# The first LayerNorm of an encoder block: rows normalized by ScalarE in one pass, factor and offset applied behind the transposes

## The chip, the cores and the metric

One core of a Trainium2 chip. The metric is the device time of one execution in microseconds (us), the median of the runs shown; lower is better. Engines are named as the profile names them: PE (TensorE), PEld (its weight loads), DVE (VectorE), ACT (ScalarE), POOL (GpSimd), SP (SyncE, which here only issues DMAs).

## What is computed

One encoder layer on 256 tokens of width 1024, in float32. Cut to what the change touches:

```python
h = layer_norm(x, ln_in_g, ln_in_b)          # 256 x 1024
mem_n = layer_norm(mem, ln_mem_g, ln_mem_b)
mix = mixer_branches(h, mem_n, ...)          # h @ w_in + b_in, three branches, gates, w_out, + b_out
h = layer_norm(DN_ALPHA * h + mix, ln1_g, ln1_b)
ff = moe_ffn(h, ...)                         # top-4 of 32 experts
out = layer_norm(DN_ALPHA * h + ff, ln2_g, ln2_b)
```

## The kernel before

The kernel has two halves. `mixer` runs from the start to about 306 us. It multiplies the transposed rows with the columns of `w_in` and with the branch weights. Each float32 operand is split into a high part (`hi`, rounded by ACT) and a low part (`lo`, the remainder, by DVE; both in `split`, L117 and L118), and `mm3` (L144 to L146) makes three matmuls of each product. `moe` runs after that and streams 403 MB of expert weights through ring buffers of 2 MB on the SP queue; the first units of the ring are loaded from inside the mixer (`early_load`).

The work around the change, in order:

- **The first LayerNorm** (L230 to L301). The 256 rows come as two tiles `xs[0]` and `xs[1]` of 128 x 1024, with factor `g` and offset `b` spread over 128 partitions (512 KB each). DVE makes the statistics; POOL raises the variance to -1/2 (L63) and DVE refines it (L69 to L74). Then each row tile is finished in pieces: ACT and POOL do columns 768 to 1023 (L283 to L285), DVE columns 0 to 511 (L287, L290) and 512 to 767 (L293, L294). The result `hs[tau]` is the normalized row tile with factor and offset; it is kept for the residual.
- **The transposes.** PE turns blocks of 128 x 128 of `hs` into PSUM tiles `tps` of 128 x 512 (one for each half `j` of the columns and each row tile `tau`), and `split` takes each straight from PSUM into `hT`.
- **The first matmuls.** The strip `wlr` of `w_in` (32 columns, its parts split at the end of the start) is multiplied with `hT` in 24 matmuls into `pj`; then follow the chunks of 128 columns of `w_in`, 24 matmuls each.
- **Small vectors.** `brow` gathers biases and LayerNorm vectors as 74 rows of 128; PE transposes it (L366) so that `bT` holds each as a column per partition.
- **The memory's LayerNorm** (`mem_norm_gen`, `mem_turn_gen`) already has the other form: ACT normalizes whole rows, and behind the transposes four ACT instructions (L399) put factor and offset on, since there they are one value per partition.
- **The residual** (`residual_gen`, L662). ACT multiplies `hs` by ALPHA (L665) and POOL adds `b_out` (L666).
- **The end of the mixer** (`ev_o`). DVE adds the projection to `hs`, makes the statistics and normalizes (L771, L772) while POOL computes the power.

Background work is written as generators that are stepped between the chunks of the matmuls (`bg.tick`); each `yield` names a number of microseconds of background work, which paces the generators. In the start, in the last projection and in the expert half the order on DVE and PE is written by hand (`manual_schedule`, which at the start takes ACT too); elsewhere a scheduler orders each engine's queue by its own model. Each engine runs its queue strictly in order. The weights in `wraw` have 3 buffers, the split parts `whi` and `wlo` 4 each, so ACT and DVE can run several chunks ahead of PE.

## Time and profile before

| | us |
|---|---|
| median of 3 runs | 1235.38 (1235.21 to 1237.03) |
| the profiled execution: its own time | 1235.43 |
| its span, first to last instruction | 1233.5 |
| busy: PE, DVE, ACT, POOL | 1168.8, 381.5, 259.0, 47.4 |
| moved by DMA | 458.24 MB |

The profiled execution lies 0.05 us from the median, and its span 1.9 us below its own time. Busy time is summed over the whole span; which engine waits for which differs by stage, so the stages are read one by one.

### The profile page before, as it was taken

The numbers are of one execution on the slowest core, as the hardware profiler recorded it, in microseconds if no ns is written. First come the engines' busy times: TensorE is split into PE (matmuls) and PEld (weight loads), VectorE is DVE, ScalarE is ACT, GpSimd is POOL, SyncE is SP. The second block draws the span as 40 slices with busy tenths as digits, with TensorE's granted clock in tenths as the row PEclk, the third lists the DMA queues.
The fourth block names the chain that finished last, engine by engine and source line by source line (L and its number), as shares of the span: only waits on it lengthen the run. The fifth ranks groups of instructions, "written<-read, shape, count | busy, mean of one in ns | idle before, by whom it ended". The sixth has DMA issues, their size and how long they took to land.

```text
span 1233.5 us, 14884 instructions
## 1 busy us (share of the span) xinstructions
PE 1168.8 (95%) x6413; PEld 639.0 (52%) x6413; DVE 381.5 (31%) x591; ACT 259.0 (21%) x453; POOL 47.4 (4%) x70
## 2 busy tenths in 40 slices
PE   7999999999999999999998989899989989898995
PEld 6898999998533443434333343334342424242432
DVE  7995565487212131120202121012111111111124
ACT  4775555453111010100101010201010101010110
POOL 2150000000000000000000000000000000000000
PEclk8999999999999999999999999899999999999998
DMA  8755557687999999999999999999999999999993
GB/s 283 258 195 172 188 196 247 257 308 271 372 378 431 425 431 431 428 431 431 430 430 432 431 430 430 431 430 430 430 430 430 431 430 430 431 429 431 429 421 129
DMA packets 74921, 458.24 MB, mean 371 GB/s; under 512 B 4662, under 2 KB 39040, under 8 KB 50148
## 3 DMA queue, kind: packets, MB, share of 16 engines
q1 hardware_dynamic: 74392, 456.62, 90.1%
q8 instruction: 52, 0.85, 0.3%
q10 hardware_dynamic: 332, 0.56, 0.2%
q14 instruction: 17, 0.14, 0.0%
q0 software_dynamic: 128, 0.07, 0.0%
HBM read 456.18 MB, written 1.05 MB: 371 GB/s over the span
## 4 chain that ended last, share of the span: by engine, by line
PE 66%; DMA 29%; DVE 2%; ACT 1%; issue 0%; SPq 0%; POOL 0%; DVEq 0%; ACTq 0%
DMA wexp<-in_w_down_dram 25%; PE gps L1004 19%; PE yps L1004 13%; PE pj L146 7%; PE pj L144 7%; PE pj L145 6%; PE mps L847 5%; DMA wexp<-in_w_gu_dram 3%; PE gps L998 2%; PE yps L1074 1%; PE mps L1074 1%; PE gps L1043 1%; DVE wlo L118 1%; PE yps L998 0%; PE mps L1121 0%
## 5 line engine op out<-in xcount | busy, mean ns | idle before, releaser
L1004 PE MATMUL gps<-wexp,xT 128*64 128x512 f32 x1984 | 441.6, 596 | 7.1 <-DMA wexp<-in_w_gu_dram 7.0
L1004 PEld LDWEIGHTS gps<-wexp,xT 128*64 128x64 f32 x1984 | 145.3, 137 | 299.0 <-issue 280.9
L1004 PE MATMUL yps<-wexp,work 128*64 128x512 f32 x960 | 234.5, 622 | 32.3 <-DMA wexp<-in_w_down_dram 32.3
L1004 PEld LDWEIGHTS yps<-wexp,work 128*64 128x64 f32 x960 | 71.4, 142 | 192.7 <-issue 143.8
L809 DVE TENSOR_SCALAR sg<-gps 128x512 f32<-128x512 f32 x31 | 21.3, 687 | 424.1 <-PE gps L1004 390.8
L118 DVE TENSOR_TENSOR wlo<-wraw,whi 128x1024 fp32r<-128x1024 f32 (+2 forms) x98 | 119.3, 1227 | 61.8 <-ACT whi L117 61.1
L810 ACT ACTIVATE sg<-sg 128x512 f32<-128x512 f32 x32 | 20.2, 630 | 460.0 <-DVE sg L809 459.9
L117 ACT ACTIVATE whi<-wraw 128x1024 fp32r<-128x1024 f32 (+2 forms) x98 | 95.4, 978 | 97.4 <-PE pj L145 80.2
L144 PE MATMUL pj<-hT,whi 128*128 128x256 f32 (+1 forms) x392 | 112.5, 287 | 0.0
L145 PE MATMUL pj<-hT,whi 128*128 128x256 f32 (+1 forms) x392 | 110.5, 282 | 0.3 <-DVE hT L118 0.3
L146 PE MATMUL pj<-hT,wlo 128*128 128x256 f32 (+1 forms) x392 | 110.5, 282 | 0.0
L1050 DVE SCALAR_TENSOR_TENSOR y<-yps,sw,y 128x512 fp32r<-128x512 f32 x30 | 22.5, 751 | 230.3 <-ACT y L1049 229.3
L145 PEld LDWEIGHTS pj<-hT,whi 128*128 128x128 f32 (+1 forms) x392 | 73.6, 188 | 1.0 <-DVE hT L118 0.8
L144 PEld LDWEIGHTS pj<-hT,whi 128*128 128x128 f32 (+1 forms) x392 | 73.6, 188 | 0.8 <-ACT whi L117 0.7
L146 PEld LDWEIGHTS pj<-hT,wlo 128*128 128x128 f32 (+1 forms) x392 | 73.5, 188 | 0.2
L1049 ACT ACTIVATE y<-yps,sw 128x512 fp32r<-128x512 f32 x30 | 20.6, 687 | 233.5 <-PE yps L1004 226.0
L847 PEld LDWEIGHTS mps<-P,h 128*128 128x128 f32 x512 | 61.6, 196 | 12.7 <-issue 12.2
L847 PE MATMUL mps<-P,h 128*128 128x128 f32 x512 | 64.8, 285 | 0.4 <-DVE P L840 0.4
L1078 DVE TENSOR_TENSOR sum<-sum,yps 128x512 f32<-128x512 f32 (+1 forms) x30 | 18.8, 666 | 71.6 <-PE yps L1074 71.6
L995 POOL COPY sel<-kp 128x128 f32<-128x128 f32 x32 | 9.4, 295 | 806.4 <-PE yps L998 450.5
L938 ACT ACTIVATE xT<-mps 128x512 f32<-128x512 f32 x32 | 19.1, 597 | 58.9 <-PE mps L847 58.9
L812 DVE TENSOR_TENSOR sg<-sg 128x512 f32<-128x512 f32 x32 | 22.1, 690 | 3.2 <-ACT sg L810 1.6
(275 smaller groups left out, 1045.9 us busy)
## 6 DMA issues: line engine op xcount, KB each, us to landing
wexp<-in_w_gu_dram SPq DMA_DIRECT2D x127, 2048.0 KB, 35.5
wexp<-in_w_down_dram SPq DMA_DIRECT2D x60, 2048.0 KB, 29.0
wraw<-in_w_in_dram SPq DMA_DIRECT2D x28, 1024.0 KB, 5.4
wexp<-in_w_down_dram SPq DMA_DIRECT2D x8, 768.0 KB, 17.3
wraw<-in_w_mem_kv_dram SPq DMA_DIRECT2D x4, 1024.0 KB
wraw<-in_w_br_gla_dram SPq DMA_DIRECT2D x4, 1024.0 KB
wraw<-in_w_out_dram SPq DMA_DIRECT2D x4, 1024.0 KB, 7.5
wraw<-in_w_br_fnet_dram SPq DMA_DIRECT2D x2, 1024.0 KB
```

The lines of the kernel that those rows point to most:

```text
L117: K.nc.scalar.activation(hi, src, AF.Copy)
L118: K.nc.vector.tensor_tensor(lo, src, hi.bitcast(F32), ALU.subtract)
L144: nc.tensor.matmul(out, wh, xh, start=first, stop=False)
L145: nc.tensor.matmul(out, wh, xl, start=False, stop=False)
L146: nc.tensor.matmul(out, wl, xh, start=False, stop=last)
L809: nc.vector.tensor_scalar(g, gate, 7.0, None, ALU.min)
L812: nc.vector.tensor_tensor(g, g, s, ALU.mult)
L847: nc.tensor.matmul(t[:, c], h1[tau][:, f0 + c % 2:f0 + 256:2], P[:, tau].rearrange("p e s -> p (e s)"), start=first and c == 0, stop=last, ...
L998: nc.tensor.matmul(ac, t[r].rearrange("k e s -> k (e s)"), bias[r, c0:c0 + ac.shape[-1]], start=first, stop=not first, skip_group_check=True)
L1004: nc.tensor.matmul(acc[e * 64:e * 64 + 64], xT[:, k, e * 64:e * 64 + 64], w[e], start=first, stop=last, skip_group_check=True)
L1050: nc.vector.scalar_tensor_tensor(y[:, 1, sl], acc, w, y[:, 0, sl].bitcast(F32), ALU.mult, ALU.subtract)
L1074: nc.tensor.matmul(c, G[:, tau * 128:tau * 128 + 128], y[:, i, sl], start=i == 0, stop=i == 1)
```

## The change

- The first LayerNorm's rows are normalized by ACT alone, one instruction of 128 x 1024 per row tile, without factor and offset. The DMAs of `g` and `b` and the pieces on DVE and POOL go.
- `brow` grows to 90 rows, with the first LayerNorm's factor and offset in rows 74 to 89, and its transpose moves to the start. Four of its pieces now come by DMAs from ACT's queue, four from POOL's; the two of `blr` go to POOL's as well.
- Behind each group of transposes a new function `turn_affine` puts factor and offset on, block by block of 128 x 128: blocks 0 and 2 on ACT, 1 and 3 on DVE, into a tile of SBUF from which `split` then takes both parts. The split of `wlr` moves behind the four turns. The memory's rows use the same function, on ACT alone as before.
- `hs` now lacks factor and offset. The residual is finished later, on DVE: `b_out`, the factor and the offset come by three DMAs of 512 KB from POOL's queue, and five DVE instructions of 128 x 1024 take the place of two of ACT and two of POOL. The residual's `yield`s now count 6 us instead of 0.
- At the end of the mixer the first of the two normalizing instructions is cut in two halves of 512 columns.

```diff
-    xs, g, b = [first[:, 0], first[:, 1]], first[:, 2], first[:, 3]
+    xs = [first[:, 0], first[:, 1]]
...
-    nc.sync.dma_start(g, A["ln_in_g"][None, :].broadcast_to([128, D]))
-    nc.sync.dma_start(b, A["ln_in_b"][None, :].broadcast_to([128, D]))
...
+    def turn_affine(x, tau, T, j, gc, bc, t, both):
+
+        ps = K.ps.tile([128, 4, 128], F32, name="tps", tag="ms")
+        for c in range(4):
+            nc.tensor.transpose(ps[:, c], x[:, (j * 4 + c) * 128:(j * 4 + c + 1) * 128], K.ident)
+        for c in range(4):
+            ga, ba = [bT[:, o + j * 4 + c:o + j * 4 + c + 1] for o in (gc, bc)]
+            if both and c % 2:
+                V.tensor_scalar(t[:, c], ps[:, c], ga, ba, ALU.mult, ALU.add)
+            else:
+                act.activation(t[:, c], ps[:, c], AF.Identity, bias=ba, scale=ga)
+        sl = slice(tau * 128, tau * 128 + 128)
+        split(K, t, T.hi[j][:, :, sl], T.lo[j][:, :, sl])
...
-            act.activation(hs[tau][:, c], xs[tau][:, c], AF.Identity, bias=t, scale=rs_[tau])
-            gp.tensor_tensor(hs[tau][:, c], hs[tau][:, c], g[:, c], ALU.mult)
-            gp.tensor_tensor(hs[tau][:, c], hs[tau][:, c], b[:, c], ALU.add)
-            c = half[0]
-            V.scalar_tensor_tensor(hs[tau][:, c], xs[tau][:, c], mvs[tau][:, 0:1], g[:, c], ALU.subtract, ALU.mult)
...
+            V.scalar_tensor_tensor(t, m[:, 0:1], -1.0, r, ALU.mult, ALU.mult)
+            act.activation(hs[tau], xs[tau], AF.Identity, bias=t, scale=r)
+        psb = K.ps.tile([128, 90], F32, name="psb", tag="ms")
+        nc.tensor.transpose(psb, brow, K.ident[:90, :90])
+        V.tensor_copy(bT, psb)
+        for j in range(2):
+            for tau in range(2):
+                t = first[:, 2 + j, tau * 512:tau * 512 + 512].rearrange("p (c n) -> p c n", c=4)
+                turn_affine(hs[tau], tau, hT, j, 74, 82, t, True)
         wlr_parts = [K.wspl.tile([128, 1024], F32R, name=n, tag=n)[:, :384].rearrange("p (k n) -> p k n", k=8)
...
-        for j in range(2):
-            for tau in range(2):
-                transpose_split(K, hs[tau], tau, hT, j)
...
+        for i, src in ((1, A["b_out"]), (2, A["ln_in_g"][None, :]), (3, A["ln_in_b"][None, :])):
+            late_rows.append(at_part(i, (D,), part3))
+            nc.gpsimd.dma_start(late_rows[-1], src.broadcast_to([128, D]))
...
-        for tau in range(2):
-            nc.scalar.activation(hs[tau], hs[tau], AF.Copy, scale=ALPHA)
-            nc.gpsimd.tensor_tensor(hs[tau], hs[tau], bo, ALU.add)
-            yield 0
+        bo, g, b = late_rows
+        nc.vector.scalar_tensor_tensor(bo, b, ALPHA, bo, ALU.mult, ALU.add)
+        yield 1.2
+        for tau in range(2):
+            nc.vector.scalar_tensor_tensor(hs[tau], hs[tau], ALPHA, g, ALU.mult, ALU.mult)
+            yield 1.2
+            nc.vector.tensor_tensor(hs[tau], hs[tau], bo, ALU.add)
+            yield 1.2
...
-                nc.vector.scalar_tensor_tensor(hs[tau], hs[tau], mv_[:, 0:1], g1, ALU.subtract, ALU.mult)
+                for c in (slice(0, 512), slice(512, D)):
+                    nc.vector.scalar_tensor_tensor(hs[tau][:, c], hs[tau][:, c], mv_[:, 0:1], g1[:, c], ALU.subtract,
+                                                   ALU.mult)
```

**The start.** ACT's queue before the change, from the normalized columns to the first chunk of weights; `h_68` and `h_69` are the two row tiles `hs`, and the brackets name the semaphore that the instruction waits for.

```order
L283 ACTIVATE h_68<-first,nmr,rsy 128x256 [waits DMAHW0_49,DVE_49]
L283 ACTIVATE h_69<-first,nmr,rsy 128x256 [waits DMAHW4_49,DVE_49]
L117 ACTIVATE whi<-wraw 128x8x32 [waits DMAHW5_49]
L117 ACTIVATE whi<-wraw 128x8x16
L117 ACTIVATE hT<-tps 128x4x128 [waits PE_49] x4
L117 ACTIVATE whi<-wraw 128x1024 [waits DMAHW6_49]
```

ACT's queue with the change, from the rows over the first of the four turns to the start of the second, and the end of the fourth.

```order
L294 ACTIVATE h_68<-first,nmr,rsy 128x1024 [waits DMAHW0_49,DVE_49]
L294 ACTIVATE h_69<-first,nmr,rsy 128x1024 [waits DMAHW4_49,DVE_49]
L278 ACTIVATE first<-tps,bT 128x128 [waits DVE_49,PE_49]
L278 ACTIVATE first<-tps,bT 128x128 [waits DVE_49]
L117 ACTIVATE hT<-first 128x4x128 [waits DVE_49]
L278 ACTIVATE first<-tps,bT 128x128 [waits PE_49]
...
L117 ACTIVATE hT<-first 128x4x128 [waits DVE_49]
L117 ACTIVATE whi<-wraw 128x8x32 [waits DMAHW7_49]
L117 ACTIVATE whi<-wraw 128x8x16
```

DVE's queue with the change at the same place, the first and the fourth turn; the two L276 of a turn are its blocks 1 and 3.

```order
L297 COPY bT<-psb 128x90 [waits PE_49]
L276 TENSOR_SCALAR first<-tps,bT 128x128 [waits Activation_49] x2
L118 TENSOR_TENSOR hT<-first,hT 128x4x128 [waits Activation_49]
...
L276 TENSOR_SCALAR first<-tps,bT 128x128 [waits Activation_49] x2
L118 TENSOR_TENSOR hT<-first,hT 128x4x128 [waits Activation_49]
L118 TENSOR_TENSOR wlo<-wraw,whi 128x8x32 [waits DMAHW7_49,Activation_49]
L118 TENSOR_TENSOR wlo<-wraw,whi 128x8x16 [waits Activation_49]
```

Before, each of the four `hT<-tps` on ACT waited for PE alone, and the split of `wlr` stood ahead of them. Now a block on one engine waits for the block before it on the other, and the split of `wlr` stands last.

**The residual on POOL.** POOL's queue before, around 58 to 86 us; `gla` holds the decayed queries and keys of the gated attention, `parts` a scratch tile.

```order
L581 MEMSET parts 128x512 [waits DVE_49,Activation_49]
L581 MEMSET parts 128x512
L482 TENSOR_TENSOR gla<-gla,parts 128x1024 [waits DMASW1_49,DMASW2_49,DMASW0_49,DMASW3_49,PE_49,Activation_49]
L483 TENSOR_TENSOR gla<-gla,parts 128x1024 [waits Activation_49,Pool_49]
L581 MEMSET parts 128x512 [waits DVE_49]
L581 MEMSET parts 128x512
L666 TENSOR_TENSOR h_68<-h_68,parts_116 128x1024 [waits DMAHW3_49]
L666 TENSOR_TENSOR h_69<-h_69,parts_116 128x1024
L482 TENSOR_TENSOR gla<-gla,parts 128x1024 [waits Activation_49]
L483 TENSOR_TENSOR gla<-gla,parts 128x1024 [waits Activation_49]
```

The same stretch of POOL's queue with the change.

```order
L610 DMA parts_114<-in_b_out_dram 128x1024 [waits DMASW2_49,DVE_49]
L575 MEMSET parts 128x512 [waits DVE_49,Activation_49]
L575 MEMSET parts 128x512
L474 TENSOR_TENSOR gla<-gla,parts 128x1024 [waits DMASW1_49,DMASW6_49,DMASW0_49,DMASW7_49,PE_49,Activation_49]
L475 TENSOR_TENSOR gla<-gla,parts 128x1024 [waits Activation_49,Pool_49]
L575 MEMSET parts 128x512 [waits DVE_49]
L575 MEMSET parts 128x512
L474 TENSOR_TENSOR gla<-gla,parts 128x1024 [waits Activation_49]
L475 TENSOR_TENSOR gla<-gla,parts 128x1024 [waits Activation_49]
```

The two L666 are gone, and the second L482 and L483 (now L474 and L475) follow the memsets directly.

**The residual on DVE.** DVE's queue with the change, around 152 us of the run before; L62 to L74 refine the second row tile's power for the gated attention, and `parts_114` holds `b_out`, factor and offset.

```order
L62 TENSOR_SCALAR ve<-oss 128x4 [waits Activation_49]
L71 TENSOR_TENSOR rst<-rsy 128x4 [waits Pool_49]
L72 TENSOR_TENSOR rst<-rst,ve 128x4 [waits DVE_49]
L660 SCALAR_TENSOR_TENSOR parts_114<-parts_114 128x1024 [waits DMASW3_49,DMASW2_49]
L73 TENSOR_SCALAR rst<-rst 128x4 [waits DVE_49]
L118 TENSOR_TENSOR wlo<-wraw,whi 128x1024 [waits PE_49,Activation_49]
L74 TENSOR_TENSOR rsy<-rsy,rst 128x4 [waits DVE_49]
L682 SCALAR_TENSOR_TENSOR parts<-pj,bT,parts 128x256 [waits Activation_49]
L606 TENSOR_TENSOR parts<-parts,rsy 128x1024 [waits DVE_49]
```

L660, which waits for two DMAs of POOL's queue (`DMASW`), now stands in front of a chunk's `wlo`; the four others of the residual (two L663, two L665) follow within the next 13 rows of that queue.

## Rows read from the trace of the kernel before

**Rows 1.** The page: the chain that ended last, by engine

```profile
PE 66%; DMA 29%; DVE 2%; ACT 1%; issue 0%; SPq 0%; POOL 0%; DVEq 0%; ACTq 0%
```

**Rows 2.** Windows: us; PE, PEld, DVE, ACT, POOL busy; granted clock; DMA share; GB/s

```profile
320.00:330.00 10.00, 10.00 (x48) 3.34 (x48) 0.00 (x0) 0.54 (x1) 0.00 (x0) 1.00 0.77 290
...
560.00:1200.00 640.00, 600.13 (x2815) 238.10 (x2816) 104.62 (x173) 59.17 (x126) 6.56 (x22) 0.97 1.01 430
```

**Rows 3.** Waits of PE from 20 to 310 us: total, times, longest

```profile
PE pj L146 <- DVE wlo L118: 0.4, 2, 0.2
```

**Rows 4.** Timeline of the start: start, length, engine, line, operation, [idle before]

```profile
4.90 4.64 PE L272 MATMUL idle<-kp 128*128 128x128 f32 x20 [4.90 <-DMA kp<-in_c_keep_dram]
...
8.24 0.21 DVE L69 SCALAR_TENSOR_TENSOR rst<-rsy,ve 128x1 f32<-128x1 f32 x1
8.40 0.55 POOL L63 TENSOR_TENSOR rsy<-ve,mh 128x1 f32<-128x1 f32 x1 [1.54 <-DVE ve L62]
...
8.87 0.16 DVE L282 SCALAR_TENSOR_TENSOR nmr<-bmv,rsy 128x1 f32<-128x1 f32 x1
9.06 0.60 ACT L283 ACTIVATE h<-first,nmr,rsy 128x256 f32<-128x256 f32 x1 [7.03 <-DVE nmr L282]
...
13.54 0.62 ACT L117 ACTIVATE whi<-wraw 128x256 fp32r<-128x256 f32 x2 [1.51 <-DMA wraw<-in_w_in_dram]
...
17.09 2.47 DVE L118 TENSOR_TENSOR hT<-tps,hT 128x512 fp32r<-128x512 f32 x4
...
18.66 0.41 PE L146 MATMUL pj<-hT,wlo 128*48 128x256 f32 x1
...
21.77 0.23 PE L366 MATMUL psb<-kp,brow 74*128 74x74 f32 x1
```

**Rows 5.** Windows of the start: columns as in rows 2

```profile
17.50:19.80 2.30, 1.96 (x10) 1.43 (x9) 2.30 (x5) 1.92 (x4) 2.30 (x5) 0.50 0.56 150
19.80:22.00 2.20, 2.20 (x21) 2.20 (x19) 2.07 (x3) 2.20 (x3) 0.71 (x2) 1.00 1.05 367
```

**Rows 6.** Durations: by form (mean ns after the bar); L399's shortest, median, longest ns

```profile
L386 ACT ACTIVATE m<-m,nmr,rsy 128x1024 f32<-128x1024 f32 x2 | 2.5, 1248 | 0.4 <-DVE nmr L385 0.3
L399 ACT ACTIVATE parts<-tps,bT x16: 437/484/528, 61.8 to 69.9; 128x128 f32<-128x128 f32 x16
L428 ACT ACTIVATE gla<-gla 128x512 f32<-128x512 f32 x4 | 2.3, 632 | 0.0
L449 DVE TENSOR_SCALAR parts<-pj,bT 128x256 f32<-128x256 f32 x4 | 1.8, 477 | 2.1 <-PE pj L146 2.1
```

**Rows 7.** Timeline from 72 to 90 us: POOL, DVE, and PE at a wait

```profile
72.96 6.02 POOL L666 TENSOR_TENSOR h<-h,parts 128x1024 f32<-128x1024 f32 x2 [2.64 <-DMA parts<-in_b_out_dram]
...
74.47 15.67 DVE L118 TENSOR_TENSOR wlo<-wraw,whi 128x1024 fp32r<-128x1024 f32 x7
...
82.84 0.28 PE L144 MATMUL pj<-mTh,whi 128*128 128x256 f32 x1
82.96 0.28 PE L145 MATMUL pj<-mTl,whi 128*128 128x256 f32 x1
83.46 0.39 PE L146 MATMUL pj<-mTh,wlo 128*128 128x256 f32 x1 [0.22 <-DVE wlo L118]
```

**Rows 8.** Timeline around 153 us, ACT and DVE

```profile
153.09 1.06 ACT L117 ACTIVATE whi<-wraw 128x1024 fp32r<-128x1024 f32 x1 [1.05 <-PE pj L145]
...
155.38 1.22 DVE L118 TENSOR_TENSOR wlo<-wraw,whi 128x1024 fp32r<-128x1024 f32 x1
```

**Rows 9.** DMA issues of the first 60 us: queue, count, size, median us to landing

```profile
first<-in_ln_in_g_dram SPq DMA_DIRECT2D x1, 512.0 KB, 5.0
...
gla<-in_w_decay_f_dram POOLq DMA_DIRECT2D x1, 32.0 KB, 4.7
```

**Rows 10.** Timeline of DVE at the end of the mixer

```profile
307.46 1.27 DVE L771 SCALAR_TENSOR_TENSOR h<-h,bmv,g 128x1024 f32<-128x1024 f32 x1
309.18 0.22 DVE L69 SCALAR_TENSOR_TENSOR rst<-rsy,ve 128x1 f32<-128x1 f32 x1 [0.45 <-POOL rsy L63]
```

More of the change, by code (lines that the diff above doesn't have):

```diff
@@ L239, in mixer @@
     chan, amask = cm[:, 0:128], [cm[:, 128:256], cm[:, 256:384]]
-    brow = one.tile([74, 128], F32, name="brow")
-    bT = one.tile([128, 74], F32, name="bT")
+    brow = one.tile([90, 128], F32, name="brow")
+    bT = one.tile([128, 90], F32, name="bT")
     blr = one.tile([48, 1], F32, name="blr")
@@ L298, in mixer @@
             split(K, wlr[:, :, fr], *[t[:, :, to] for t in wlr_parts])
-        for j in range(2):
-            for tau in range(2):
-                transpose_split(K, hs[tau], tau, hT, j)
     tc.no_sync_barrier()
@@ L569, in mixer @@
     omT, yfT = [Split([small[:, i]], [small[:, i + 1]]) for i in (0, 2)]
+    late_rows = []
     def inner_gen():
```

51 lines of the change are left out of this document (15 added, 36 removed).

## The prediction, made before the changed kernel ran

> **What bounds the kernel now.** I read the chain that ended last, then windows over the expert half, then PE's waits, then the start.
>
> The chain goes through PE for 66% and through DMAs for 29% [rows 1], so the question is where each of the two rules. From 560 to 1200 us the 16 DMA engines are busy all the time, share 1.01 at 430 GB/s, and PE waits for weights [rows 2]. There the end is set by the bytes still to come, not by any instruction. But shortly after the expert half begins the share is 0.77: PE works without a pause and DMA waits for a ring buffer that PE has yet to free [rows 2]. So when the stream becomes continuous hangs on when PE gets there. A microsecond that PE gains or loses before 320 us moves the whole stream, and the end, by a microsecond.
>
> Before 320 us I ask whether PE has slack. From 20 us to the end of the mixer it waits in only two places that the profile names, 0.4 us in all, for DVE's `wlo` [rows 3]. So PE is packed, and the time at which it starts its dense work is handed on to the end. It starts at the 24 matmuls of `wlr`: the third stands at 18.66, and the stream has passed on to L366 at 21.77 [rows 4].
>
> **The start, step by step.** Everything up to the first row tile's `nmr` stays, so ACT can begin its rows at 9.06, 0.03 us after `nmr` ends (8.87 + 0.16); that 0.03 is the price of a handover between DVE and ACT [rows 4]. The second `nmr` no longer stands behind a factor multiply. Its power is there at 8.95 (8.40 + 0.55), and the four small instructions take what the first four took, 8.24 to 9.03, so it is ready at about 9.85 [rows 4]: earlier than ACT needs it. ACT's two instructions of 128 x 1024 cost 1.25 us each by the same form in the memory's LayerNorm [rows 6]. ACT is through with the rows at 9.06 + 2 x 1.25 = 11.55, and with successive instructions overlapping by about 0.1 I start the first block at 11.45. The row tiles' transposes are in time for that, since the first row tile is ready at 10.3.
>
> Then come the four turns, and the order decides. ACT's block 0, DVE's block 1, ACT's block 2, DVE's block 3 each wait for the one before, `hT`'s high part waits for block 3, the low part for the high part. Nothing of one turn runs beside anything else of it. Prices: a block on ACT 0.44 us (the shortest of 16 of the same form, which is the one that did not queue) [rows 6]. A block on DVE does not occur before: 256 columns out of PSUM with a scalar operand took 0.48, half of that is 0.24 [rows 6], and as each instruction has a fixed part I take 0.35 between the two. The high part, 512 columns out of SBUF on ACT, 0.63 by L428 [rows 6]. The low part on DVE 0.62 (a quarter of 2.47) [rows 4], 0.60 to the next start. Handovers 0.03 each.
>
> The first turn reaches the end of its high part after 0.44 + 0.35 + 0.44 + 0.35 + 0.63 + 4 x 0.03 = 2.33 us, at 13.8. In the next one, ACT's block 0 lies beside DVE's low part, so a turn's period is 0.03 + 0.60 + 0.35 + 0.03 + 0.44 + 0.03 + 0.35 + 0.03 + 0.63 = 2.49. Three of them: the fourth high part ends at 13.8 + 7.5 = 21.3. Behind it ACT splits `wlr` (0.62 [rows 4]), to 21.9, and DVE follows to 22.5. The third matmul, L146, which needs `wlo`, starts at 22.55 instead of 18.66: **3.9 later**.
>
> The clock adds to that. From L146 to L366 the run before takes 3.1 us, partly at the lower level (0.50 granted to 19.8, then 1.00 [rows 5]). With the change PE has nothing to do from the last transposes, around 13, until 22. After its first idle stretch, from 9.5, the granted clock was down when it came back [rows 4, 5], and the dense run of `idle` matmuls at the very start kept the slow spacing throughout: 4.64 us for 20, 0.22 each (less the 0.4 of the last one's own length) [rows 4]. So I price the 22 matmuls from L146 on at the lower level: 22 x 0.22 = 4.8 instead of 3.1, **1.7 more**. Together the start costs 5.6. The bounds: with blocks of 0.24 on DVE a turn takes 2.27 and the start costs 4.7; with 0.48 on DVE 2.75 and 6.6; with the clock at the upper level from 22 us on 2.2 less (22 x 0.12 instead of 22 x 0.22); with the clock low for another 2 us behind the strip 1 more.
>
> A rule speaks to these handovers. The Trainium skill, "PSUM — Partial Sum Buffer", section "PSUM bank collisions raise a hardware error", says that two engines may not touch one PSUM bank in the same partitions at the same time, two readers included, and that a dependency is put between them even where they touch different columns. By that rule sharing the blocks of one `tps` between ACT and DVE can't gain from working side by side, and the sum is the 5.6 above; without it the two would overlap, which is the first rival. That the waits stand there is in the order; what they cost, no row of the run before shows.
>
> **What else moves.** The two DMAs of `g` and `b` leave SP's queue (5.0 us to landing for the first [rows 9]); that frees the loads of `wlr` and of the chunks to come earlier, but they are not what the start waits for any more, so nothing. `brow` now gates PE from 9.5 on. POOL issues six DMAs from about 1.1 us; at 4.7 us to landing [rows 9] and some 0.5 to 0.7 us each to issue, the fourth lands at about 8, inside the cover of the `idle` run (to 9.5 [rows 4]); if it took 3 us more it would cost 1 to 2.
>
> POOL's L666, 6.0 us long, runs beside DVE's `wlo`: seven of these took 15.67 us, 2.2 each, where one alone takes 1.22 [rows 7, 8]. That has made PE wait: from 82.96 to the next matmul 0.50 us where the spacing is 0.12 [rows 7], and once more the same a chunk later (the two waits of rows 3). With small gaps beside them I make that 1.0 us, and without L666, DVE is some 3.2 us further (two `wlo` at their lone price), so **1.0 back**. Bounds 0 and 3.2.
>
> The five late instructions on DVE, about 1.25 each, 6.2 us, go where DVE has idle time; the first waits for DMAs that POOL issues around 150 us, which land some 5 us later [rows 9]. Behind it stands a `wlo` (155.38 in the run before [rows 8]). ACT's `whi` of that chunk could start only when PE let go of a buffer at 153.09 [rows 8]; with four buffers three chunks, some 8 us, lie ahead of it on PE, so about 5 us of lateness cost nothing. I take 0; if the DMAs came 10 us late it would cost 2 to 3. Removing ACT's 2 us of scaling at 20 us gives nothing, as PE waits for ACT nowhere there [rows 3].
>
> Cutting L771: the power on POOL ends 0.45 us after DVE's 1.27 us instruction is through [rows 10]. If POOL gets in between the halves, up to 0.4 come back; **0.1** taken.
>
> Sum: +5.6 - 1.0 - 0.1 = +4.5 on the profiled execution's own 1235.43 (0.05 from the median): **1239.9 us**.
>
> **The rivals.** One: the handovers cost little, because the two engines overlap after all. Then a turn is ACT's side alone, 2 x 0.44 + 0.63; four take 6.0, to 17.5, `wlr`'s low part is ready at 18.7, and L146 starts when it did. The start costs between nothing and the 1.7 of the clock; with the 1.0 and 0.1 that is 1234.3 to 1236, and 1233.5 if ACT's instructions overlap by a further 0.1 each. For it speaks that each engine touches only its own blocks; against it, the waits in both queues. This is the case that ends on the other side, and it decides from where a turn takes under 1.4 us (4.5 us less over four).
>
> Two: DVE's relief is worth its whole 3.2 us. The Trainium skill, "SBUF — State Buffer", section "Who interferes with whom", has a `tensor_tensor` with two SBUF inputs contend with a GpSimd instruction that reads SBUF; `wlo` beside L666 agrees (2.2 against 1.22). If all of it reached PE, the sum is 5.6 - 3.2 - 0.1: 1237.7, no change. Against it: PE lost only about 1 us there.
>
> Three: worse than forecast, by the clock staying low into the first chunk, a late `brow`, or a late residual: 1 to 3 us more, 1241 to 1243.
>
> **Numbers.** 0.2%, 2.5 us, is about what a measurement of this kernel can tell from no change. Forecast 0.62 (nearly all slower by more than that), rival one 0.10 (a third of it faster, the rest the same), two 0.12 (the same, mostly, and if rival one's price met it, faster), three 0.16. Faster 0.05, same 0.18, slower 0.77. The range is 1236.8 to 1242.6: below lies rival one, above the worst of three.
>
> **What would show it.** In the changed trace: ACT's L278 and DVE's L276 strictly alternating, a turn every 2.5 us; the last `hT` on ACT near 21; the first L144 after 21.5; spacing of 0.21 to 0.22 there, 0.12 later; no PE wait for `wlo` at 83 to 87 us after its shift; DMA windows after 560 unchanged at 430 GB/s. I am wrong if the turns overlap, or if PE's lateness at 22 us is no longer there at 306.

## The result, and the profile after

The changed kernel takes 1245.37 us (median of 4 runs, 1243.39 to 1246.05) where the kernel before took 1235.85 beside it: ratio 1.0071, 95% interval 1.0058 to 1.0083. That is 9.5 us slower, on the side forecast, but outside the range; the forecast was 1239.9. The profiled execution of the changed kernel took 1246.05, its span is 1244.3.

The timeline of the start, which answers to [rows 4]:

```profile
9.10 0.16 DVE L293 SCALAR_TENSOR_TENSOR nmr<-bmv,rsy 128x1 f32<-128x1 f32 x1
9.29 2.37 ACT L294 ACTIVATE h<-first,nmr,rsy 128x1024 f32<-128x1024 f32 x2 [7.26 <-DVE nmr L293]
10.58 3.92 PE L272 MATMUL tps<-kp,h 128*128 128x128 f32 x16 [0.80 <-ACT h L294]
11.73 0.46 ACT L278 ACTIVATE first<-tps,bT 128x128 f32<-128x128 f32 x1
12.23 0.41 DVE L276 TENSOR_SCALAR first<-tps,bT 128x128 f32<-128x128 f32 x1 [2.05 <-ACT first L278]
12.67 0.46 ACT L278 ACTIVATE first<-tps,bT 128x128 f32<-128x128 f32 x1 [0.48 <-DVE first L276]
13.16 0.41 DVE L276 TENSOR_SCALAR first<-tps,bT 128x128 f32<-128x128 f32 x1 [0.53 <-ACT first L278]
13.61 0.63 ACT L117 ACTIVATE hT<-first 128x512 fp32r<-128x512 f32 x1 [0.48 <-DVE first L276]
14.14 0.44 ACT L278 ACTIVATE first<-tps,bT 128x128 f32<-128x128 f32 x1
14.27 0.69 DVE L118 TENSOR_TENSOR hT<-first,hT 128x512 fp32r<-128x512 f32 x1 [0.70 <-ACT hT L117]
14.88 0.40 DVE L276 TENSOR_SCALAR first<-tps,bT 128x128 f32<-128x128 f32 x1
15.32 0.46 ACT L278 ACTIVATE first<-tps,bT 128x128 f32<-128x128 f32 x1 [0.73 <-DVE first L276]
...
21.55 0.63 ACT L117 ACTIVATE hT<-first 128x512 fp32r<-128x512 f32 x1 [0.48 <-DVE first L276]
...
22.74 0.45 PE L144 MATMUL pj<-hT,whi 128*48 128x256 f32 x1 [8.23 <-ACT whi L117]
22.82 0.62 DVE L118 TENSOR_TENSOR wlo<-wraw,whi 128x256 fp32r<-128x256 f32 x2
...
23.50 0.45 PE L146 MATMUL pj<-hT,wlo 128*48 128x256 f32 x1
```

ACT and DVE take turns, block by block, each released by the other (the brackets name DVE on ACT and ACT on DVE). The four high parts stand at 13.61, 16.26, 18.91 and 21.55: a turn every 2.65 us. PE stood still for 8.23 us. Its third matmul is at 23.50; before it was at 18.66.

The windows of the strip, which answer to [rows 5]:

```profile
22.00:28.00 6.00, 5.17 (x23) 4.41 (x24) 3.59 (x5) 3.53 (x6) 3.06 (x6) 0.50 0.57 181
28.00:30.90 2.90, 2.90 (x26) 2.89 (x25) 2.51 (x4) 1.06 (x1) 0.00 (x0) 1.00 1.10 389
```

PE runs the whole strip at the lower level, 23 matmuls in the 5.3 us from 22.74; the first chunk then starts at 28.13 (21.80 before) and goes at the upper level.

PE's waits from 20 us to 318 us, which answer to [rows 3] (the 8.2 us are the start):

```profile
PE pj L144 <- ACT whi L117: 8.2, 1, 8.2
PE pdps L648 <- DVE ab L639: 0.5, 1, 0.5
PE pj L146 <- DVE wlo L118: 0.2, 1, 0.2
```

One of the two waits for `wlo` is gone; one for `ab`, DVE's part of the Fourier branch, is new. And at the end of the mixer, which answers to [rows 10], DVE goes on at once behind the cut instruction:

```profile
310.81 1.41 DVE L771 SCALAR_TENSOR_TENSOR h<-h,bmv,g 128x512 f32<-128x512 f32 x2
312.13 0.21 DVE L69 SCALAR_TENSOR_TENSOR rst<-rsy,ve 128x1 f32<-128x1 f32 x1
```

In the expert half, which answers to [rows 2], nothing has changed in kind; the chain goes through PE for 65% and DMAs for 31% (66% and 29% in [rows 1]):

```profile
320.00:330.00 10.00, 9.60 (x78) 8.33 (x79) 5.24 (x31) 4.23 (x9) 0.58 (x2) 1.00 0.99 423
560.00:1200.00 640.00, 599.54 (x2836) 240.52 (x2832) 106.03 (x174) 61.09 (x128) 6.62 (x22) 0.98 1.01 430
```

**What these rows don't show.** I laid the matmuls of the mixer side by side, each with the same one of the other trace. At the first chunk the changed kernel is 6.33 us late, at the first expert matmul 8.57 (328.40 against 319.83). Waits explain only a few tenths of that growth. The rest comes in evenly, some 0.03 us with each chunk of 24 matmuls. The row that shows it is the window from 215 to 275 us, instructions of `pj` alone; first the kernel before:

```profile
215.00:275.00 60.00, 60.00 (x508) 60.00 (x507) 6.90 (x10) 4.16 (x10) 1.00 0.77 286
```

and the changed kernel:

```profile
215.00:275.00 60.00, 60.00 (x502) 60.00 (x502) 5.61 (x9) 5.05 (x12) 1.00 0.72 260
```

Both are at the upper clock and PE is never idle, yet PE gets through six fewer of the same matmuls of 256 columns. Less the two that hang over the window's ends, that is one every 118.6 ns before and one every 120.0 after. Nothing in the forecast answers to this.

### The profile page after: what moved, and what is told of

Its sections match the earlier page's. It is cut to its first block, busy times and chain, and to the rows that moved or that the text cites. A ratio compares the mean times of both kernels' runs of the same rounds, so it can differ in the third digit from the quotient of the medians.

```text
span 1244.3 us, 14894 instructions
## 1 busy us (share of the span) xinstructions
PE 1172.2 (94%) x6413; PEld 641.9 (52%) x6413; DVE 381.2 (31%) x598; ACT 261.9 (21%) x459; POOL 40.4 (3%) x73
## 4 chain that ended last, share of the span: by engine, by line
PE 65%; DMA 31%; DVE 3%; ACT 1%; issue 1%; SPq 0%; POOL 0%; DVEq 0%; ACTq 0%
DMA wexp<-in_w_down_dram 30%; PE gps L1005 17%; PE yps L1005 13%; PE pj L146 7%; PE pj L144 7%; PE pj L145 7%; PE mps L848 5%; PE gps L999 2%; PE yps L1075 1%; PE mps L1075 1%; PE gps L1044 1%; DVE wlo L118 0%; DMA first<-in_x_dram 0%; PE gps L952 0%; PE yps L999 0%
## 5 line engine op out<-in xcount | busy, mean ns | idle before, releaser
L118 DVE TENSOR_TENSOR wlo<-wraw,whi 128x1024 fp32r<-128x1024 f32 (+2 forms) x98 | 116.0, 1190 | 59.3 <-ACT whi L117 58.9
L146 PE MATMUL pj<-hT,wlo 128*128 128x256 f32 (+1 forms) x392 | 111.9, 285 | 0.3 <-DVE wlo L118 0.2
L146 PEld LDWEIGHTS pj<-hT,wlo 128*128 128x128 f32 (+1 forms) x392 | 73.6, 188 | 1.2 <-DVE wlo L118 0.9
L848 PEld LDWEIGHTS mps<-P,h 128*128 128x128 f32 x512 | 61.6, 196 | 12.7 <-issue 12.2
```

Of the source, the lines that this page charges most:

```text
L118: K.nc.vector.tensor_tensor(lo, src, hi.bitcast(F32), ALU.subtract)
L146: nc.tensor.matmul(out, wl, xh, start=False, stop=last)
L848: nc.tensor.matmul(t[:, c], h1[tau][:, f0 + c % 2:f0 + 256:2], P[:, tau].rearrange("p e s -> p (e s)"), start=first and c == 0, stop=last, ...
```

## The experiments

The measure that I use beside the times is the start of the first expert matmul, since executions of one kernel agree in it to about a microsecond (319.83 and 320.13 before, 328.40 and 327.19 with the change), while whole executions of the kernel before lay between 1233.9 and 1239.6 on one chip. All 19 traces take 899.2 to 901.7 us from the first expert matmul to the last, without any order by kernel, so what the mixer loses the end loses, within these 2.5 us, as the forecast had it. (The two profiled executions of the first pair differ by 10.6 us, of which 2.0 arise behind the first expert matmul; in the second pair the expert half took 1.1 less with the change.)

**1. Both kernels once more.**

> The kernel before once more, for a second trace. In the two traces so far successive matmuls of 256 columns stand 118.6 ns apart before and 119.9 ns after, all through the mixer, though neither engine nor operands differ; over the mixer that makes about 2 us of the 10.8 us between the two profiled executions. If the spacing goes with the execution or the chip and not with the program, this trace and that of the changed kernel taken beside it show the same spacing, whichever it is (equal to within 0.3 ns). If it goes with the program, 118.6 here and 119.9 there.

> The changed kernel once more, beside the kernel before on the same chip. Start theory (the alternation of ACT and DVE and the lower clock behind it cost 6.3 us before 28 us; the spacing of the matmuls belongs to the execution): the first expert matmul stands 6.5 to 7.5 us later than in the trace of before taken beside it, not 8.6, and the ratio stays at 1.006 to 1.008. Rival (the late rows in the residual slow PE by 1% all through the mixer): 8.6 again.

The spacing went with the program: steps of 117.3 and 118.7 ns in the kernel before against 119.9 to 120.0 in the changed one, as in the first pair. My expectation, that it belonged to the execution, fell. First expert matmul 320.13 and 327.19, 7.06 apart; of the 1.5 us less than in the first pair, 1.1 lie ahead of the first chunk, where the clock came back at 26.33 instead of 28.00 in the changed kernel and at 20.50 instead of 19.82 in the other. Ratio 1.0072 (1.0052 to 1.0092), time 1244.44 against 1235.77.

**2. The residual alone.** As in the change, three late DMAs from POOL's queue (not shown here) and five instructions on DVE.

```diff
...
-        bo = at_part(1, (D,), part3)
-        late(bo, A["b_out"].broadcast_to([128, D]))
-            nc.scalar.activation(hs[tau], hs[tau], AF.Copy, scale=ALPHA)
-            nc.gpsimd.tensor_tensor(hs[tau], hs[tau], bo, ALU.add)
-            yield 0
+        bo, g, b = late_rows
+        nc.vector.scalar_tensor_tensor(bo, b, 0.0, bo, ALU.mult, ALU.add)
+        yield 1.2
...
+            nc.vector.scalar_tensor_tensor(hs[tau], g, 0.0, hs[tau], ALU.mult, ALU.add)
+            yield 1.2
+            nc.vector.scalar_tensor_tensor(hs[tau], hs[tau], ALPHA, bo, ALU.mult, ALU.add)
+            yield 1.2
```

> The kernel before with the residual as the change has it: three late DMAs from POOL's queue, five DVE instructions of 128 x 1024, the same yields; L666 on POOL and L665 on ACT gone. As hs is complete here, factor and offset of the late rows are taken times zero, so the result is the reference's. Start theory: PE gains 0.3 to 0.9 us at 83 to 90 us and loses 0.7 us at the wait for DVE's ab near 171 us, so 1235.2 to 1236.2, ratio 0.9995 to 1.0004. Rival (the residual carries what the start's 6.3 us leave of the 9.5 us): 1238 to 1239, ratio 1.002 to 1.003.

1236.82 against 1235.77, ratio 1.0002 (0.9992 to 1.0013), first expert matmul at 320.67. The rival falls: the residual doesn't carry the missing 3 us. Inside, the terms differ from what I expected: PE gained 0.4 at the `wlo` and lost 1.5, not 0.7, around the Fourier branch (1.3 of it in one wait for DVE's `ab`); and from 207 us on the matmuls stood 117.4 ns apart instead of 118.7, which gave 0.9 back. So the spacing can change within one program, in steps.

**3. Idle matmuls in PE's pause.**

```diff
+        idle = K.ps.tile([128, 128], F32, name="idle", tag="ms")
+        for _ in range(48):
+            nc.tensor.matmul(idle, K.ident, K.ident, start=True, stop=True)
         wlr_parts = [K.wspl.tile([128, 1024], ...
```

> The changed kernel with 48 further idle matmuls of 128 columns on PE between the last transposes (14.1 us) and the strip's matmuls (22.7 us), so that PE has work all through its pause. Clock theory (the granted clock is 0.50 from 17.8 to 28.0 us because PE stood still, and the strip's 24 matmuls stand 0.213 us apart for it): the clock stays at 1.00, the strip goes at 0.12 spacing, the first chunk starts at about 25.8 instead of 28.1, time 2.3 us less, about 1243.1. Rival (the clock would be low there anyway, or the strip waits for its operands): no change, 1245.4. If the 48 last beyond 22.7 us, up to 1 us is lost.

The 48 lasted 10.98 us, to 24.39, longer than I had reckoned, and so pushed the strip back by 1.6; the first chunk came at 27.27, not at 25.8. But the granted clock was 1.00 from 9.57 us on, and the strip took 2.88 us instead of 5.39 and 4.61. The window of this strip, to be held against the one from 22 to 28 us above:

```profile
24.30:27.20 2.90, 2.90 (x27) 2.90 (x27) 1.75 (x2) 1.25 (x2) 1.97 (x4) 1.00 0.91 262
```

The first expert matmul stood at 327.38, where the same kernel without them had 327.19: gain and delay cancel. That the clock falls with PE's pause and costs the strip about 2 us is shown; the time, 1247.1, shows no gain (its six executions lie at 1243.1 and 1244.0, and at 1247.0 to 1247.4; I don't know why).

**4. Sharing the blocks.** Two PSUM tiles for a turn, and all blocks on ACT:

```diff
-        ps = K.ps.tile([128, 4, 128], F32, name="tps", tag="ms")
+        ps = [K.ps.tile([128, 4, 128], F32, name="tps", tag="ms") for _ in range(2 if both else 1)]
+        at = lambda c: ps[c % 2 if both else 0][:, c]
```

```diff
-                turn_affine(hs[tau], tau, hT, j, 74, 82, t, True)
+                turn_affine(hs[tau], tau, hT, j, 74, 82, t, False)
```

> The changed kernel with the four blocks of a turn in two PSUM tiles, ACT's two in one and DVE's two in the other, so that no block waits for one on the other engine; the order on each engine is kept. Bank theory (the alternation costs the start its 5.2 us): a turn then is two blocks on both engines side by side (0.8), the high part (0.63), and the low part (0.62) that stands ahead of the next blocks on DVE, 2.1 us instead of 2.65; the strip's first matmul at about 20.5 instead of 22.8, and the first expert matmul 2.2 us earlier than the changed kernel's 327.2 to 328.4. Rival (the waits between the engines cost little, the work itself is what is long): the turn stays at 2.5 or more, and nothing moves by more than 0.6.

> The changed kernel with all four blocks of a turn on ACT, as for the memory's rows. Bank theory: the handovers go, a turn is four blocks at about 0.4 and the high part, 2.1 to 2.2 us, with the low part beside the next turn; the strip's first matmul at 20.8 to 21.0. Rival (sharing the blocks halves the time as it is meant to): a turn longer than 2.65, the strip later than 22.8.

Two turns of two_banks; blocks 0 and 2 on ACT and 1 and 3 on DVE now lie side by side:

```profile
14.01 0.79 ACT L279 ACTIVATE first<-tps,bT 128x128 f32<-128x128 f32 x2
14.13 0.69 DVE L118 TENSOR_TENSOR hT<-first,hT 128x512 fp32r<-128x512 f32 x1 [1.04 <-ACT hT L117]
14.74 0.72 DVE L277 TENSOR_SCALAR first<-tps,bT 128x128 f32<-128x128 f32 x2
...
15.56 0.63 ACT L117 ACTIVATE hT<-first 128x512 fp32r<-128x512 f32 x1 [0.76 <-DVE first L277]
...
17.65 0.63 ACT L117 ACTIVATE hT<-first 128x512 fp32r<-128x512 f32 x1 [0.76 <-DVE first L277]
```

A turn takes 2.09 us (2.1 expected). On ACT alone it takes 2.05, a little under the 2.1 to 2.2 expected: one engine doing all four blocks is faster than two that share them in one tile (2.65). From ACT's first row to the strip's first matmul it is 10.55 us with two tiles and 11.33 on ACT alone, 13.45 and 13.26 in the two traces of the change. Both started 0.6 to 1.1 us later than those, since the second row tile landed later (see 8), and so the strip stood at 20.93 and 21.43, not at 20.5 and 20.8 to 21.0, and the first expert matmul at 326.83 and 326.45, 0.4 to 2.0 ahead of the change's and not 2.2. Times: 1242.52 (ratio 1.0043, 1.0027 to 1.0058) and 1244.68 in a single execution. The bank theory holds: in the changed kernel the handovers, not the work, make a turn long. (Two tiles are two banks here; whether a second tile in the same bank would do as well was not tried.)

**5. The place of the split tiles.** The wider `bT` (90 columns for 74) moves all small tiles behind it by 64 bytes, and with them `whi` and `wlo`, which hold the parts of the weights. By the allocation (the addresses in the built program) they lie at 96 from a multiple of 128 bytes before, at 32 with the change. The edits: the wider tiles alone in the kernel before (wide_rows); a pad ahead of the two (only_splits_moved), which moves besides them only `g1` and `b1`, factor and offset that PE doesn't read; and other widths of `bT` in either kernel.

```diff
-    brow = one.tile([74, 128], F32, name="brow")
-    bT = one.tile([128, 74], F32, name="bT")
+    brow = one.tile([90, 128], F32, name="brow")
+    bT = one.tile([128, 90], F32, name="bT")
```

```diff
+    pad = K.wspl.tile([128, 16], F32, name="pad", tag="pad", bufs=1)
+    nc.gpsimd.memset(pad, 0.0)
```

> The kernel before with only brow and bT as wide as in the changed kernel (90 instead of 74), of which the added part stays unused: the tiles allocated behind them, whi and wlo among them, lie 64 bytes further on. The matmuls of 256 columns stand 117.4 or 118.7 ns apart in the kernel before and 120.0 ns in the changed one, each the same in two executions, and the residual alone left them at 118.7 and then 117.4. Address theory: 120.0 ns here as well, and the first expert matmul 2 to 2.5 us later than before's 319.8 to 320.1. Rival (the spacing comes from what PE did before, or from the other engines): 117.4 or 118.7 ns, and 320.1.

> The kernel before with a tile of 64 bytes ahead of whi and wlo in their own pool, so that these two alone lie 64 bytes further on; bT, lrT and the other small tiles stay (POOL fills the added tile, 0.1 us at its start). If it is the place of whi and wlo that sets the spacing: 120.0 ns all through and the first expert matmul at 322.4 to 322.7, as with wide_rows. Rival (one of the other tiles that had moved there, lrT or bT): 117.3 to 118.8 ns and 319.8 to 320.4.

> The changed kernel with bT another 16 columns wider, which stay unused: whi and wlo then lie 128 bytes behind their place in the kernel before, at the same distance from a multiple of 128 bytes (96) as there, and not at 32 as in the changed kernel. Address theory: the matmuls of 256 columns stand 117.4 to 118.8 ns apart instead of 120.0, the first expert matmul comes 2.0 to 2.4 us earlier than the changed kernel's (327.2 in the run with the earlier clock), at about 325, and the time falls to 1242 to 1243. Rival (the step of 64 bytes made a difference in the kernel before only): 120.0 ns and 327.2.

> The kernel before with bT 24 columns wider, unused: whi and wlo at 64 from a multiple of 128 bytes, the place not yet seen. Address theory: another spacing than 120.0, the same all through the mixer but for the steps of 1.3 ns after interruptions; first expert matmul between 317.5 and 322.6.

> The kernel before with whi and wlo at 64 from a multiple of 128 bytes once more, timed: its one look had 117.8 ns in the first part and 113.3 from about 195 us on, and the first expert matmul at 315.28. Place theory: the same spacings and 315.3 again, time 1232 to 1234 where before has 1235.5 to 1237.5, ratio 0.996 to 0.9975. Rival (an execution's own luck): 118.7 ns, 320, ratio 1.000.

The same window, first of wide_rows, then of tiles_back, then of before_at_64_timed:

```profile
215.00:275.00 60.00, 60.00 (x502) 60.00 (x501) 6.81 (x10) 4.16 (x10) 1.00 0.77 280
```

```profile
215.00:275.00 60.00, 60.00 (x517) 60.00 (x516) 6.22 (x9) 5.03 (x12) 1.00 0.73 269
```

```profile
215.00:275.00 60.00, 60.00 (x532) 60.00 (x531) 7.60 (x11) 3.35 (x9) 1.00 0.78 292
```

| kernel | `whi`, `wlo` at | spacing, ns | first expert matmul | time; ratio |
|---|---|---|---|---|
| before | 96 | 117.3 to 118.8 | 319.83, 320.13 | |
| wide_rows, one execution | 32 | 120.0 | 322.55 | 1238.64 |
| only_splits_moved, one execution | 32 | 120.0 | 322.42 | 1240.12 |
| the change | 32 | 120.0 | 328.40, 327.19 | 1.0071 |
| tiles_back | 96 | 116.7 | 324.46 | 1240.91; 1.0029 (1.0017 to 1.0041) |
| before_at_64, one execution | 64 | 117.8, then 113.3 | 315.28 | 1232.90 |
| before_at_64_timed | 64 | 117.8, then 113.3 | 315.11 | 1232.26; 0.9964 (0.9950 to 0.9977) |

The address theory holds in all five as far as 120.0 goes: it stands at 32 and not at 96 or 64, and moving the split tiles is enough. How fast the other places are it did not say rightly: tiles_back has 116.7 where 117.4 to 118.8 was expected, and before_at_64 a step of 4.5 ns and 315.28 where I had expected steps of 1.3 ns and 317.5 at the least. The wide rows alone cost 2.42 us at the first expert matmul, against the second trace of the kernel before, of which 0.21 were there at the first chunk already: 2.2 us for 64 bytes that hold nothing. tiles_back stands 2.7 and 3.9 ahead of the change's two traces, although its first chunk came later (29.08). But from its first chunk to the first expert matmul it takes 295.4 us and the kernel before, also at 96, 298.0, so its ratio of 1.0029 is not the price of the change without the place: some 2.6 us are in it that the better spacing gives. The kernel before, with 24 unused columns and no other edit, becomes 0.36% faster. What is not explained: at one place there are steps (117.4 and 118.7 in the kernel before, 116.7 in tiles_back, 117.8 and 113.3 at 64), which change only after an interruption, such as transposes between two chunks. In the three programs traced twice they came out the same in both executions, but for two stretches of the kernel before: from 22 us 118.7 in one and 117.3 in the other, from 87 us the other way round. So whether the spacing is 120.0 or less goes with the program; which of the lower steps a stretch gets does not always.

**6. Another start.** The change's form, with the first tile's power refined ahead of the second one's statistics, two PSUM tiles, DVE's blocks ahead of the low part of the turn before, the strip's split between the turns, and idle matmuls.

```diff
+        spin(9)
+        mv0 = ln_stats(K, xs[0])
+        r0 = Rstd(K, mv0[:, 1:2], LN_EPS, 1)
+        norm(0, mv0, r0)
...
+        turn(0, 0)
+        turn(0, 1)
+        t00 = blocks(0, 0)
+        hi_of(0, 0, t00)
+        norm(1, mv1, r1)
+        lo_of(0, 0, t00)
+        spin(8)
+        turn(1, 0)
+        turn(1, 1)
...
+        t10 = blocks(1, 0)
+        hi_of(1, 0, t10)
+        t01 = blocks(0, 1)
+        lo_of(1, 0, t10)
+        for to, fr in ((slice(0, 32), slice(0, 32)), (slice(32, 48), slice(16, 32))):
+            split(K, wlr[:, :, fr], *[t[:, :, to] for t in wlr_parts])
```

> The changed kernel with another start: the first row tile's power is refined ahead of the second one's statistics (the tile has landed 2.5 us before the second), factor and offset come as 16 rows of their own at the head of POOL's queue, blocks 0 and 1 of a turn on ACT and 2 and 3 on DVE in two PSUM tiles, DVE's blocks of the next turn ahead of the low part, the strip's split between the turns, and 16 idle matmuls to keep PE at work. Residual and end as in the change. Bank and clock theory: the strip's first matmul at 15.5 to 17, its 24 matmuls at 0.12 spacing, the first chunk at 18.5 to 20 against 21.8 to 22.1 before; the first expert matmul at 316 to 319 (before 319.8 to 320.1), time 1232 to 1236, so the first version that could beat before. Rival (the form itself is slow, as each row goes through three passes): first chunk later than 22, time over 1237.

1238.47 against 1237.14 (ratio 1.0012, 1.0003 to 1.0021). The strip started at 16.27 and the first chunk at 20.11, 1.7 to 2.0 us ahead of the kernel before, a little later than the 18.5 to 20 expected because the strip waited once more for a low part. But `whi` lay at 32 here, the spacing was 120.0, and the first expert matmul stood at 321.03. The form isn't slow in itself; the rival falls on the first chunk, and its time of over 1237 comes from the place.

**7. Start and place together.** The same with an unused width added to the small tile that holds factor and offset.

```diff
-    gT = one.tile([128, 16], F32, name="gT")
+    gT = one.tile([128, 24], F32, name="gT")[:, :16]
```

24 columns put `whi` and `wlo` at 64, 32 at 96, 40 at 0.

> The start of reordered_start, with whi and wlo at 96 from a multiple of 128 bytes as in the kernel before (they were at 32 in reordered_start, and its matmuls 120.0 ns apart). Address theory: first chunk at 20.1 as there, first expert matmul at 318.6 to 319.0 instead of 321.03, 1.1 to 1.5 us ahead of before; time 1235.5 to 1236.2 where before has 1237.1, ratio about 0.999. Rival: 321.0, ratio 1.001.

> The same with whi and wlo on a multiple of 128 bytes. If what counts is how far a 128-byte row of weights reaches over such a boundary, the spacing is the shortest here, 117.4 ns or less throughout, and the first expert matmul at 317 to 318.6; if 96 is merely another place with no order in it, 117.4 to 120.0.

> The start of reordered_start with whi and wlo at 64. Start and place are two terms that add: the start brings the first chunk to 20.1 (before 21.8 to 22.1), the place the spacing. If 113.3 ns holds from about 195 us on as in before_at_64, the first expert matmul stands at 313.5 to 315.0 and the time is 1230.5 to 1232.5; if 117.8 ns holds throughout, 317.2 and 1235. Rival (they don't add, as the expert half takes its time from the weight stream): over 1235 in both.

At 96 the spacing was 116.7, not 118.7, so the first expert matmul came at 316.35, earlier than expected; 1234.33 against 1237.52, ratio 0.9975 (0.9965 to 0.9985). At 0 my guess fell: 120.0, and 320.81, ratio 1.0001 (0.9992 to 1.0010); only where `whi` is the operand that streams, in matmuls of 512 columns, was 0 the best place (227 to 228 ns, 233 to 234 at 96). At 64: 113.3 in the first four chunks, then 117.8, and 113.3 again from 188 us; first expert matmul 313.16, **1231.37 against 1236.28, ratio 0.9958 (0.9944 to 0.9972)**, the version that beats both kernels. Most of that is the place: beside the same runs of the kernel before, before_at_64_timed alone has 0.9964, and the two intervals overlap, so that the times by themselves don't show a gain from the start. Its start, against the change's above:

```profile
7.57 1.24 ACT L295 ACTIVATE h<-first,nmr,rsy 128x1024 f32<-128x1024 f32 x1 [5.53 <-DVE nmr L294]
...
11.14 1.24 ACT L295 ACTIVATE h<-first,nmr,rsy 128x1024 f32<-128x1024 f32 x1
...
14.27 1.95 PE L289 MATMUL idle<-kp 128*128 128x128 f32 x16
...
15.97 0.36 PE L144 MATMUL pj<-hT,whi 128*48 128x256 f32 x1
...
19.76 0.36 PE L144 MATMUL pj<-hT,whi 128*128 128x256 f32 x1
```

At the first expert matmul start and place add, as nearly as can be read: it stands 1.95 us ahead of before_at_64_timed, with a first chunk 2.08 earlier (19.76 against 21.84). The change's residual and end, and the 113.3 of the first stretch (some 0.4 us), are in the 1.95 too. In the times 0.9 of it is left.

**8. The second row tile.** DVE began its statistics at 6.3 to 6.6 us in the seven traces with the loads of before, and at 6.8 to 7.9 in the six with the change's loads and its order, with the same DMA issued at 1.7. (The expectation below counts four more, those of the reordered start; there DVE isn't free before 7.4 to 7.7, so they tell nothing of the landing.) What differs on SP's queue: without the two loads of 512 KB, and with fewer on ACT's queue, the strip's load is issued at 2.16 instead of 6.9, and runs beside it.

```diff
     nc.sync.dma_start(xs[1], A["x"][0, 128:256])
+    nc.sync.dma_start(brow[58:66], A["ln_mem_g"].rearrange("(c p) -> c p", p=128))
```

> The changed kernel with one of the small loads of brow (4 KB, the memory's factor) moved from POOL's queue to SP's, behind the second row tile. With it, the load of the strip (512 KB) waits for the first row tile's landing and is issued at 4.5 us; in the changed kernel it is issued at 2.16, and DVE starts the second row tile's statistics at 6.8 to 7.9 in ten traces, against 6.3 to 6.6 in seven with the start of before, where two loads stand ahead of it and it goes at 6.7 to 7.0. Load theory (the strip's load takes bandwidth from the second row tile): statistics at 6.4 to 6.8, the strip's first matmul at 22.2 to 22.7 instead of 22.7 to 23.6, time about 0.7 us less than the changed kernel's, 1243.7. Rival (POOL's small loads, or chance): 6.8 to 7.9 as before.

> reordered_at_64 with the strip's load held in the same way. There the second row tile's statistics began at 7.60 and its turns set when the strip ends. Load theory: statistics at about 7.0 (DVE is busy with the first tile's power to 7.5, so at least there), the first chunk at 19.1 to 19.6 instead of 19.76, first expert matmul at 312.5 to 313.0, time 1230.5 to 1231.2. Rival: nothing, since DVE isn't free before 7.5 anyway: 19.76 and 313.2, 1231.4.

Held to 4.21, the strip's load left the second tile's statistics at 6.79, at the lower end; the strip at 22.70, 1244.49 (1.0061, 1.0045 to 1.0077). The two starts are within what was expected, the time is not (1243.7), and the statistics lie 0.04 us from the earliest trace without the hold, so it doesn't decide. In the other DVE was busy up to its statistics at 7.80, so they tell nothing; the first chunk came at 20.23 and the first expert matmul at 313.75, not earlier than 19.76 and 313.16: no gain, 1231.09 (0.9953, 0.9939 to 0.9967). What delays the tile stays open; that it came later whenever the change's loads were there, is what thirteen traces show.

## Why the prediction was wrong

The direction and the main mechanism were right, and about half of the time was missing. Terms at the first expert matmul, forecast and measured (first pair of traces; second pair in brackets):

| term | forecast | measured |
|---|---|---|
| start, to the first chunk | +5.6 | +6.33 (+5.27) |
| DVE's relief at 80 to 95 us | -1.0 | -0.2 (-0.2) |
| late residual on DVE | 0 | +0.8 (+0.3) |
| cut of L771 | -0.1 | -0.4 (-0.4) |
| place of `whi` and `wlo` | not in the sum | +2.2 |
| sum | +4.5 | +8.7 (+7.2); traces +8.57 (+7.06) |

The three middle terms are read as changes of the distance between the traces of the change and of wide_rows, which has the same place and spacing: by the clock of wide_rows 5.73 us around 75 us, 5.50 from 88 to 171, 6.27 from 174 to the end of the chunks, 5.85 at the first expert matmul. (From 184 to 206 us the distance dips, as the two traces have the same transposes at other places between the chunks.) The times are further apart than these terms: 9.5 us in the first pair and 8.7 in the second, against 8.57 and 7.06 at the first expert matmul. The remaining 1.0 and 1.6 arise behind it or in the executions that were not traced, and stay open.

**The step that failed** is the one on what the change adds: it priced instructions, DMAs, waits and the clock, and took `brow grows to 90 rows` for a question of when the rows land. That the wider tile moves the tiles behind it, and that PE's pace depends on their place, is the 2.2 us that the sum didn't have. No row of the kernel before showed it, and no bound covered it. Two terms of the sum were mis-sized besides, both to the same side: DVE's relief by 0.8 and the late residual by 0.8 (0.3 in the second pair).

**The start** was right in its mechanism and 0.7 too small in the first pair. The third matmul is 4.84 late, not 3.9: the first block starts at 11.73 instead of 11.45 (the second row tile's landing, 0.23 later); the first turn takes 2.51 to the end of its high part instead of 2.33, and the period is 2.65 instead of 2.49, three times. DVE's block takes 0.41, between the 0.35 taken and the upper bound of 0.48, and ACT's 0.46, not 0.44. The clock's term, 1.7 forecast, was 1.5 (4.63 from L146 to the first chunk, 3.14 before); in the second pair it was 0.4, because the clock came back at another time. The sentence `so nothing` on the earlier loads of `wlr` is not confirmed, see 8.

The Trainium skill, "PSUM — Partial Sum Buffer", section "PSUM bank collisions raise a hardware error", was cited for the rule that two engines' accesses to one bank are put one behind the other. The runs agree: a turn went from 2.65 to 2.09 us when the two engines' blocks had a bank each, with the order on each engine unchanged.

**DVE's relief** was 0.2, not 1.0. Only half of the work beside `wlo` had gone (L666's 6.0 us of 12.7 on POOL): POOL's multiplications for the gated attention moved up into its place. DVE's five `wlo` there still take 1.94 us each (2.24 for seven in [rows 7]):

```profile
80.94 9.68 DVE L118 TENSOR_TENSOR wlo<-wraw,whi 128x1024 fp32r<-128x1024 f32 x5
```

and POOL's timeline beside it:

```profile
80.37 2.42 POOL L474 TENSOR_TENSOR gla<-gla,parts 128x1024 f32<-128x1024 f32 x1 [3.59 <-ACT gla L471]
82.73 3.40 POOL L475 TENSOR_TENSOR gla<-gla,parts 128x1024 f32<-128x1024 f32 x1
```

The order quoted with the change showed this: with L666 gone, the second L482 and L483 directly follow the memsets. The Trainium skill, "SBUF — State Buffer", section "Who interferes with whom", by which a `tensor_tensor` with two SBUF inputs contends with a GpSimd instruction that reads SBUF, fits here too (1.94 us against 1.22 alone); it was the overlap that I had read wrongly. The place has a part in it: with 120.0 ns between matmuls PE comes later to the `wlo`, and wide_rows, which still has L666, already lost one of the two waits (0.2 us left of 0.4). At the place of before the same relief was worth 0.4, in residual_alone. And the bound of 3.2 was not worked out rightly: two `wlo` at their lone price are 2.4.

**The late residual** was taken to cost nothing, since PE was three chunks ahead of the `wlo` behind it. It did not wait there; it waited for the second `ab`, which on DVE stands behind the last two instructions of the residual (L665) and the `wlo` that they delay. DVE's queue, and PE at the wait:

```profile
173.57 2.35 DVE L665 TENSOR_TENSOR h<-h,parts 128x1024 f32<-128x1024 f32 x2
175.84 1.22 DVE L118 TENSOR_TENSOR wlo<-wraw,whi 128x1024 fp32r<-128x1024 f32 x1
176.97 0.42 DVE L638 COPY ab<-cdps 128x252 f32<-128x252 f32 x1
177.30 0.41 DVE L639 TENSOR_SCALAR ab<-cdps 128x252 f32<-128x252 f32 x1
...
176.49 0.83 PE L648 MATMUL pdps<-parts,ab 128*128 128x129 f32 x6
177.86 1.35 PE L648 MATMUL pdps<-parts,ab 128*128 128x127 f32 x10 [0.55 <-DVE ab L639]
```

In the kernel before, `ab` was there at 168.90 and PE came for it at 169.58. In the second trace of the change DVE had the second `ab` 1.2 us earlier and PE came 0.8 earlier, and the loss was 0.3.

I had looked at one consumer behind the moved instructions, not at all of them.

**The cut of L771** gave the full 0.4 that had been named as its upper bound: L69 starts 1.39 us behind L62 instead of 1.79.

**The expert half** did what was forecast: share 1.01 at 430 GB/s, and the delay of 320 us is there at the end. The rivals: one fell with the alternation; two fell, the relief being smaller and not larger; three named one of the things that happened, a late residual; without the place the first pair's terms come to +6.4, 1241.8, which lies in it.

## What to carry to other kernels

Before sharing a tile's blocks between two engines, look at whether the tile lies in one PSUM bank: if so, each handover can cost a wait, and one engine alone can be faster, as here (2.05 us a turn against 2.65). When an edit changes the size of any tile, lay the same matmuls of both traces side by side and compare their spacing before explaining a loss by waits; and try pads of a multiple of 32 bytes ahead of the matmul's operands: here one of 96 bytes was worth 4.0 us in the kernel before, and the reordered start 1.95 at the first expert matmul. For an instruction moved onto a busy engine, list every consumer that stands behind it there, not just the nearest.

## What the runs showed of the hardware that was not expected

- Matmuls of 256 columns with unchanged operands, order and clock (1.00) stood 113.3, 116.7, 117.4, 117.8, 118.7 or 120.0 ns apart, depending on where the 128 x 1024 tiles of weights lay: always 120.0 at 32 from a multiple of 128 bytes (eight programs) and at 0 (one), never 120.0 at 96 (four) or 64 (three). Within a program it went from one of these steps to another only after an interruption, and the two executions of the kernel before stay within 0.1 us of a constant distance from 30 us to the end of the mixer. The distance from a multiple of 128 bytes is not all of it: two programs at 96 have 117.4 and 118.7, two 116.7 almost throughout.
- With idle matmuls in PE's pause the granted clock stayed at 1.00 from 9.57 us to behind the end of the mixer. Without them it was 0.50 for 7 to 14 us around the pause in five traces with the change's order, ending between 24.6 and 29.2 us, at another time in each; in the sixth (strip_load_held) the clock's records begin only at 27.07, and the strip took 4.99 us.
- The second of two loads of 512 KB on one queue was there between 6.8 and 7.9 us in six traces with the same loads, and set when the whole start could go on.
